# Turned RWKV product loops, inverses from blocks of 16, and two gate projections at another place in the order

## The chip, the cores and the metric

The kernel runs on one core of a Trainium2 chip, as one launch. The time is the device time of the launch in microseconds (us). TensorE (PE) multiplies, VectorE (DVE) and ScalarE (ACT) work elementwise and read the results out of PSUM, GpSimd (POOL) does elementwise work beside them, and SyncE (SP) issues the DMAs.

## The reference

One sequence of 512 tokens with 1024 features goes through two blocks. The first has one layer with two mixers, sparse attention (NSA, 8 heads) and RWKV-7 (8 heads of 64), each gated by a silu. The second block has two layers (differential attention, then gated linear attention), each with cross attention to a memory and a convolutional feed-forward. What the change touches is the RWKV mixer, whose reference is a scan over tokens:

```python
def rwkv7_step(state, inp):
    r_t, w_t, k_t, v_t, kk_t, a_t = inp
    sa = jnp.einsum('bhvk,bhk->bhv', state, -kk_t)
    state = (state * w_t[:, :, None, :] + sa[..., None] * (kk_t * a_t)[:, :, None, :]
             + v_t[..., None] * k_t[:, :, None, :])
    y = jnp.einsum('bhvk,bhk->bhv', state, r_t)
    return state, y
...
o_rwkv = o_rwkv * jax.nn.silu(g_rwkv.astype(jnp.float32))
```

## The kernel before

All matrix products with weights run as three half-precision products: weights and activations are split into a high and a low f16 part. `wahead` loads a weight block (128x1024 f32, `wst`) by DMA, ACT makes `whi` and DVE makes `wlo` from it. Inside a stretch named by `WPOOL` (from the first to the fifth step of `I`) `wlo` is made by POOL instead, after one more ACT pass. A 128-column projection is 24 matmuls of 512 columns into a PSUM bank `psp`: 7 with `whi`, 7 with `wlo`, 7 with the low activations, then three more.

The RWKV scan is done in chunks of 64 tokens. There are 4 pairs of heads (`f`), each with 2 heads (`hp`), and 4 blocks of 128 tokens (`tb`) with 2 chunks each (`c`); so 64 pairs of head and chunk, of which 32 stand side by side in the free dimension (`u`) and 2 in the partitions. The steps are:

- `rwkv_s1` (A0 to A3, one per `f`) makes, among others, the 64x64 matrices `LR` of each head and chunk, and at its end the first parts of `Y` and `KV`: for each `c` 16 products of 64x64 by 64 columns in f32 (lines 848 to 861), `hp` outermost, so that 8 products in a row write the same half of the partitions.
- `rwkv_inv` (I) inverts 64 unit-triangular matrices of 64x64. DVE transposes the two 32x32 diagonal blocks of each into `lx` (line 876), so that each partition holds one 32x32 system, solves them by 31 steps of forward substitution (lines 880 to 891: a product into `itmp` and a subtraction, in two groups of columns, so up to four instructions a step), and transposes back into `itmp` and `Tt` (lines 895 and 899). The block between the diagonal ones follows from small products on PE: 64 products of 32x32 by 32 columns at line 908 and 64 at line 920, in two halves each, `c` outside `u`.
- `rwkv_s2` (M) multiplies by these inverses (line 938, bank `psx` from `AX` and `Tt`) and then, for each `f` and `c`, makes 16 products of 64x64 by 64 columns into `pv` and 16 into `pv2` (lines 953 to 962), `hp` outermost.
- `rwkv_chain` (H) runs the recurrence over the 8 chunks, and `rwkv_s5` (F0 to F3) makes a gate projection, its silu (two POOL additions or products each) and the output's group norm.

Beside it run the NSA steps: K and C (keys and compressed keys), P0 to P3 (a pair of heads each: projection, scores `pss`, softmax on DVE and ACT, values `pso`) and G0 to G3 (gate projections and their silu). The list `ORDER` gives the order in which these steps are written; each entry advances its step to the next `yield`. What is written then goes through a scheduler, which moves instructions on each engine; the order that results is fixed, and each engine works it off one after the other. A wait of one instruction on PE is so a wait of everything behind it. In phase A there is one PSUM bank `x` (`psx`) and there are two of `psp`, three of `pss`.

A function `mm` (line 298) issues the matmuls; those of `rwkv_inv` are called on the engine directly and so have lines of their own. An f32 product is two records of PE in the trace (one weight load and one matmul each).

Of the kernel before, what the change touches and what calls it, by code (L numbers as in the profile page):

```python
# [18 lines left out]
NT = 4  # L19
# [7 lines left out]

ORDER = (
# [4 lines left out]
).split()  # L33
WKS = (1, 2, 6, 0, 3, 5, 4, 7)
# [2 lines left out]
DITEMS = "h0 c0 h1 h2 c1 h3 h4 h5".split()  # L37
LAG = 3
NDEPTH, NHL, NTT = 2, 3, 4
WPOOL = ('I.1', 'I.5')  # L40
DKS = (7, 1, 3, 2, 6, 4, 0, 5)
ICOLS = (0,7,32)
IPOOL = 9
GORDER = "m0 k q v0 v1 v2 m1".split()
GFILL = (4500, 1000, 0, 8500)
GKS = (1, 2, 0, 3, 6, 4, 7, 5)
# [4 lines left out]
def _const_table():  # L51

    p = np.arange(128)
    c = {}
    c["ident"] = np.eye(128)
    c["bones"] = (p[:, None] // 64 == p[None, :] // 64) * 1.0
    same = p[:, None] // 64 == p[None, :] // 64
    c["u_inc"] = same & (p[:, None] <= p[None, :])
    c["v_inc"] = c["u_inc"] / 16.0
    c["v_suf"] = (same & (p[:, None] > p[None, :])) / 16.0  # L60
# [165 lines left out]
class Kern:  # L226
# [521 lines left out]
    def rwkv_s1(self, f):  # L748
# [99 lines left out]
        for c in range(2):  # L848
            cr = slice(64 * c, 64 * c + 64)
            p = self.psx()  # L850
            pv = p.rearrange("p (a b v) -> p a b v", a=2, b=NT)
            for hp in range(2):
                rows = slice(64 * hp, 64 * hp + 64)
                for tb in range(NT):
                    vv = vT[cr, tb, 64 * hp:64 * hp + 64]
                    self.mm(pv[rows, 0, tb, :], vv, kT[cr, hp, tb, 1, :])
                    self.mm(pv[rows, 1, tb, :], khT[cr, tb, 64 * hp:64 * hp + 64], vv)
            yv = P["Y"][:, f, :].rearrange("p (b c t) -> p b c t", b=NT, c=2)
            self.act(yv[:, :, c, :], pv[:, 0], AF.Copy)
            kv = P["KV"][:, f].rearrange("p (b c) v -> p b c v", b=NT)  # L860
            self.act(kv[:, :, c, :], pv[:, 1], AF.Copy)


    def rwkv_inv(self):
        nc, ip = self.nc, self.tp
        P = self.rwt
        LR = P["LR"]
        LRu = LR.rearrange("p h b a t -> p (h b) a t")
        lx = self.T(ip, [128, 2, 32, 32], F32, "lx")
        LU, XT = lx[:, 0], lx[:, 1]  # L870
        X = XT.rearrange("p i t -> p t i")
        tmp = self.T(ip, [128, 1024], F32, "itmp")
# [4 lines left out]
        nc.gpsimd.memset(XT, 0.0)  # L877
        nc.gpsimd.memset(XT.rearrange("p a b -> p (a b)")[:, 0:1024:33], 1.0)

        for i in range(31):  # L880
            n = 31 - i
            for g, (c0, c1) in enumerate(zip(ICOLS, ICOLS[1:])):
                m = min(i + 1, c1) - c0
                if m > 0:
                    eng = nc.gpsimd if g == IPOOL else nc.vector
                    tv = tmp[:, 256 * g:256 * g + n * m].rearrange("p (a b) -> p a b", a=m)
                    self.tt(tv, LU[:, None, i + 1:, i].to_broadcast([128, m, n]),
                            XT[:, c0:c0 + m, i:i + 1].to_broadcast([128, m, n]), ALU.mult, eng)
                    self.tt(XT[:, c0:c0 + m, i + 1:], XT[:, c0:c0 + m, i + 1:], tv, ALU.subtract, eng)
            if i % 6 == 5:  # L890
                yield
        D = self.T(ip, [128, 1024], F32, "itmp").rearrange("p (u i) -> p u i", u=32)
        Tt = self.T(ip, [128, 32, 64], F32, "Tt")
        nc.gpsimd.memset(Tt, 0.0)
        nc.vector.transpose(out=D.rearrange("p u i -> p i u"), in_=X.rearrange("p t i -> p i t"))
        for q in range(4):
            r = slice(32 * q, 32 * q + 32)
            o = 32 * (q % 2)
            nc.vector.transpose(out=Tt[r, :, o:o + 32].rearrange("p u t -> p t u"), in_=X[r])
        E = LU  # L900
        for half in range(2):
            p = self.psx()
            pv = p.rearrange("p (u i) -> p u i", u=16)
            for c in range(2):
                a, b = slice(64 * c, 64 * c + 32), slice(64 * c + 32, 64 * c + 64)
                for u in range(16):
                    uu = half * 16 + u
                    self.nc.tensor.matmul(pv[b, u, :], lhsT=LRu[a, uu, 0, 32:64], rhs=D[a, uu, :], start=True,
                                          stop=True, tile_position=(64 * c, 64 * c + 32))
            for c in range(2):  # L910
                b = slice(64 * c + 32, 64 * c + 64)
                self.act(E[b, half * 16:half * 16 + 16, :], pv[b], AF.Copy)
        for half in range(2):
            p = self.psx()
            pv = p.rearrange("p (u i) -> p u i", u=16)
            for c in range(2):
                a, b = slice(64 * c, 64 * c + 32), slice(64 * c + 32, 64 * c + 64)
                for u in range(16):
                    uu = half * 16 + u
                    self.nc.tensor.matmul(pv[a, u, :], lhsT=E[b, uu, :], rhs=Tt[b, uu, 32:64], start=True, stop=True,  # L920
                                          tile_position=(64 * c + 32, 64 * c))
            for c in range(2):
                a = slice(64 * c, 64 * c + 32)
                self.act(Tt[a, half * 16:half * 16 + 16, 32:64], pv[a], AF.Copy, scale=-1.0)
        self.dump("Tt", Tt)
        self.Tt = Tt

    def rwkv_s2(self):
# [17 lines left out]
        for f in range(4):  # L946
            for c in range(2):
# [5 lines left out]
                for hp in range(2):  # L953
                    rows = slice(64 * hp, 64 * hp + 64)
                    h = 2 * f + hp
                    for tb in range(NT):
                        rb = LR[cr, h, tb, 1, :]
                        bh = Bh[cr, tb, h * 64:h * 64 + 64]
                        self.mm(pv[rows, 0, tb, :], WU[cr, h, tb, 0:64], rb)
                        self.mm(pv[rows, 1, tb, :], WU[cr, h, tb, 64:128], rb)  # L960
                        self.mm(pv2[rows, 0, tb, :], WU[cr, h, tb, 0:64], bh)
                        self.mm(pv2[rows, 1, tb, :], bh, WU[cr, h, tb, 64:128])
# [1002 lines left out]
```

## Time and profile before

| | us |
|---|---|
| three runs | 1648.43, 1652.76, 1655.37 (median 1652.76) |
| the profiled execution | 1650.08 |
| its span, first to last instruction | 1648.2 |
| PE busy | 1565.3 (95%) |
| DVE busy | 1039.3 (63%) |
| ACT busy | 759.9 (46%) |
| POOL busy | 231.4 (14%) |

PE is the busiest engine by far. Its slices in the page's second part are at 90% or more nearly everywhere; after the first slice the lowest ones are 7s, in the seventh (247 to 288 us) and the eleventh (412 to 453 us) of 40, and the line of the granted clock has an 8 and a 7 in the seventh and eighth. The seventh and eighth are the place of `rwkv_inv`. Phase A, with everything that the change touches, ends before 500 us. A line number in a row is that of the kernel before; line 298 is `mm`, 282 ACT's helper, 285 and 288 those of the two DVE (and POOL) forms.

### The profile page before, as it was taken

The page shows a single profiled execution, that of the slowest core. Times are in us where ns is not written, and L with a number is a line of the kernel's source. Part 1 is how long each engine was busy: PE and PEld are TensorE (multiplying, and loading weights), DVE is VectorE, ACT ScalarE, POOL GpSimd, SP SyncE. Part 2 cuts the span into 40 slices and gives each one's busy share as a digit, 9 for nine tenths or more (in the row PEclk, how much of TensorE's full clock was granted, in tenths as well). Part 3 has the DMA queues.
Part 4 walks back from the last instruction along what each step waited for, and adds up shares of the span by engine and source line. Part 5 has one row for each costly group of instructions (what it writes and reads, how often), then busy time and mean ns, then how long its engine had stood idle before and what let it go on. Part 6 is the DMA issues. An engine that isn't in the chain of part 4 may idle for free. (4 is left out here: it accounts for less than half of the span.)

```text
span 1648.2 us, 25438 instructions
## 1 busy us (share of the span) xinstructions
PE 1565.3 (95%) x9876; PEld 837.5 (51%) x9876; DVE 1039.3 (63%) x1908; ACT 759.9 (46%) x1399; POOL 231.4 (14%) x198
## 2 busy tenths in 40 slices
PE   6999997899799998899999999999999999999999
PEld 2465553576446665544444444456764444444444
DVE  6645779866755888876777763332476577777422
ACT  4443553454554777644444442225465444444211
POOL 2200124011141111221111110101000211111000
PEclk8999998799998999999999999999999999999999
DMA  5333441443453655533333333333224333333342
GB/s 186 99 106 97 100 103 37 87 81 72 95 162 110 162 147 129 132 98 102 100 100 101 100 102 101 106 92 97 65 59 115 103 102 103 101 101 100 111 125 64
DMA packets 133817, 171.06 MB, mean 104 GB/s; under 512 B 83471, under 2 KB 95680, under 8 KB 133697
## 3 DMA queue, kind: packets, MB, share of 16 engines
q1 hardware_dynamic: 133120, 168.39, 36.4%
q8 instruction: 77, 1.26, 0.3%
q10 hardware_dynamic: 576, 1.05, 0.2%
q14 instruction: 44, 0.35, 0.1%
HBM read 137.03 MB, written 3.28 MB: 85 GB/s over the span
## 5 line engine op out<-in xcount | busy, mean ns | idle before, releaser
L298 PEld LDWEIGHTS <-whi 128*128 128x128 f16 x3508 | 336.7, 98 | 401.4 <-issue 29.5
L285 DVE SCALAR_TENSOR_TENSOR wlo<-wst,whi 128x1024 f16<-128x1024 f32 (+2 forms) x250 | 306.9, 1228 | 255.6 <-ACT whi L282 255.0
L282 ACT ACTIVATE whi<-wst 128x1024 f16<-128x1024 f32 (+2 forms) x252 | 258.2, 1025 | 401.5 <-PE psp L298 328.6
L298 PE MATMUL psp<-hh,wlo 128*128 128x512 f16 x1112 | 296.6, 385 | 17.8 <-DVE wlo L285 17.8
L298 PE MATMUL psp<-hh,whi 128*128 128x512 f16 x1112 | 294.9, 381 | 10.6 <-ACT hh L282 6.3
L298 PE MATMUL psp<-hl,whi 128*128 128x512 f16 x1112 | 292.7, 381 | 0.0
L298 PEld LDWEIGHTS <-wlo 128*128 128x128 f16 x1754 | 170.9, 98 | 217.9 <-DVE wlo L285 19.0
L285 DVE SCALAR_TENSOR_TENSOR c<-ux,vecs,c 128x511 f32<-128x511 f32 (+1 forms) x176 | 133.2, 757 | 4.9 <-ACT c L282 1.8
L288 POOL TENSOR_TENSOR gl<-gg,gh 128x512 f16<-128x512 f32 x44 | 50.9, 1157 | 423.9 <-ACT gh L282 423.9
L298 PE MATMUL psp<-gh,wlo 128*128 128x512 f16 x352 | 91.6, 379 | 0.0
L298 PE MATMUL psp<-gl,whi 128*128 128x512 f16 x352 | 91.6, 379 | 0.0
L298 PE MATMUL psp<-gh,whi 128*128 128x512 f16 x352 | 91.6, 379 | 0.0
L288 POOL TENSOR_TENSOR acc<-acc,sq 128x512 f32<-128x512 f32 x34 | 53.0, 1564 | 220.2 <-ACT sq L282 220.2
L285 DVE SCALAR_TENSOR_TENSOR ux<-psp,rf 128x512 f32<-128x512 f32 x88 | 60.6, 688 | 32.6 <-PE psp L298 30.2
L282 ACT ACTIVATE c<-ux,vecs 128x512 f32<-128x512 f32 x88 | 70.3, 798 | 1.6 <-DVE ux L285 1.6
L282 ACT ACTIVATE c<-c 128x512 f32<-128x512 f32 x44 | 27.7, 629 | 91.6 <-DVE c L285 91.6
L298 PEld LDWEIGHTS <-hh 128*128 128x128 f16 x576 | 55.8, 98 | 19.8 <-issue 5.0
L298 PE MATMUL pso<-T,vh 128*64 128x128 f16 (+1 forms) x440 | 49.3, 224 | 13.2 <-DMA T<-hl 12.5
L282 ACT ACTIVATE pss<-pss,smst 128x128 f32<-128x128 f32 (+3 forms) x64 | 32.1, 501 | 51.1 <-DVE smst L293 45.5
L285 DVE SCALAR_TENSOR_TENSOR gg<-c,c 128x512 f32<-128x512 f32 x44 | 30.4, 692 | 34.8 <-ACT c L282 34.8
L298 PE MATMUL psp<-whi,hh 128*128 128x256 f16 (+3 forms) x240 | 51.3, 281 | 0.8 <-DVE kn L285 0.8
L298 PE MATMUL psp<-whi,hl 128*128 128x256 f16 (+3 forms) x240 | 51.7, 281 | 0.0
(452 smaller groups left out, 2230.9 us busy)
## 6 DMA issues: line engine op xcount, KB each, us to landing
wst<-in_w_up SPq DMA_DIRECT2D x88, 512.0 KB, 3.4
wst<-in_w_dn SPq DMA_DIRECT2D x32, 512.0 KB, 3.6
wst<-in_w_o SPq DMA_DIRECT2D x24, 512.0 KB, 3.6
wst<-in_w_rw SPq DMA_DIRECT2D x13, 512.0 KB, 3.3
wst<-in_w_dqk SPq DMA_DIRECT2D x12, 512.0 KB, 3.8
wst<-in_w_dn SPq DMA_DIRECT2D x16, 384.0 KB, 3.1
wst<-in_w_g SPq DMA_DIRECT2D x8, 512.0 KB, 3.6
wst<-in_w_dv SPq DMA_DIRECT2D x6, 512.0 KB, 4.2
```

The costliest lines, as they stand in the source:

```text
L282: return self.nc.scalar.activation(*a, **k)
L285: return self.nc.vector.scalar_tensor_tensor(out, in0, scalar, in1, op0=op0, op1=op1)
L288: return (eng or self.nc.vector).tensor_tensor(out, a, b, op=op)
L298: return self.nc.tensor.matmul(out, lhsT=lhsT, rhs=rhs, start=start, stop=stop, **kw)
```

## The change

Four things change. (1) The loops over 64x64 products at the end of `rwkv_s1` and in `rwkv_s2` are turned: the two heads of a pair alternate, so that neighbouring products write different halves of the partitions. The loops over 32x32 products in `rwkv_inv` are turned in the same way (`c` inside `u`). (2) The substitution works on blocks of 16 instead of 32. ACT copies the diagonal blocks into `LD` (4 copies of 32 partitions x 1024), DVE transposes them at once, 15 steps of two instructions each solve both 16x16 blocks (`r`) of a 32x32 system, and two further products on PE per system, 32x32 by 16 columns, give the block between them: 128 products at line 904 and 128 at line 914, which go round the four 32x32 quarters on the diagonal of the array. Between and around them stand two masked ACT copies (`B`, scaled by the new constant `m16`), DVE transposes, and at the end four ACT copies into `Tt`. (3) In `ORDER` F0, F1, G1 and G2 stand between the first and the second step of `I`. (4) `WPOOL` is empty: all `wlo` are made by DVE.

```diff
-    "... A3 F2 I F0 F1 I I I I P1 P1 P1 G1 P1 I P1 I "
-    "P1 P2 P1 P1 M ... P2 H P2 H G2 P2 P2 H P2 P3 "
+    "... A3 F2 I F0 F1 G1 G2 I P1 I P1 I P1 I P1 P1 "
+    "P1 P2 P1 P1 M ... P2 H P2 H P2 P2 H P2 P3 "
...
-WPOOL = ('I.1', 'I.5')
+WPOOL = ()
...
-            for hp in range(2):
-                rows = slice(64 * hp, 64 * hp + 64)
-                for tb in range(NT):
-                    vv = vT[cr, tb, 64 * hp:64 * hp + 64]
-                    self.mm(pv[rows, 0, tb, :], vv, kT[cr, hp, tb, 1, :])
-                    self.mm(pv[rows, 1, tb, :], khT[cr, tb, 64 * hp:64 * hp + 64], vv)
+            for tb in range(NT):
+                for hp, rows in halves:
+                    self.mm(pv[rows, 0, tb, :], vT[cr, tb, rows], kT[cr, hp, tb, 1, :])
+                for hp, rows in halves:
+                    self.mm(pv[rows, 1, tb, :], khT[cr, tb, rows], vT[cr, tb, rows])
...
-            nc.vector.transpose(out=LU[r], in_=LRu[r, :, 0, o:o + 32].rearrange("p u t -> p t u"))
+            self.act(LD[r], LRu[r, :, 0, o:o + 32], AF.Copy)
+        nc.vector.transpose(out=LU, in_=LD.rearrange("p u t -> p t u"))
...
-        for i in range(31):
-            n = 31 - i
...
+        for i in range(15):
+            n, m = 15 - i, i + 1
+            tv = it[:, 512:512 + 2 * n * m].rearrange("p (r a b) -> p r a b", r=2, a=m)
+            self.tt(tv, lu[:, :, None, i + 1:, i].to_broadcast([128, 2, m, n]),
+                    Xr[:, :, 0:m, i:i + 1].to_broadcast([128, 2, m, n]), ALU.mult)
+            self.tt(Xr[:, :, 0:m, i + 1:], Xr[:, :, 0:m, i + 1:], tv, ALU.subtract)
...
+        nc.vector.transpose(out=D.rearrange("p u c -> p c u"), in_=X.rearrange("p c r t -> p c (r t)"))
+        yield
+        for r in range(2):
+            self.act(B[:, :, 16 * r:16 * r + 16], D, AF.Copy, scale=m16[:, r:r + 1])
+        nc.vector.transpose(out=BT, in_=B)
...
+        for u in range(32):
+            for r, o, tp in quarters:
+                nc.tensor.matmul(pv[r, u, :], lhsT=LRu[r, u, 0, o:o + 32], rhs=B[r, u, 0:16], start=True, stop=True,
+                                 tile_position=tp)
+        self.act(E[:, :, 0:16], pv, AF.Copy, scale=m16[:, 1:2])
+        yield
...
+                nc.tensor.matmul(pv[r, u, :], lhsT=E[r, u, :], rhs=BT[r, u, 16:32], start=True, stop=True,
+                                 tile_position=tp)
+        self.tt(BT[:, :, 16:32], BT[:, :, 16:32], pv, ALU.subtract)
+        nc.vector.transpose(out=D, in_=BT)
...
+        for r, o, tp in quarters:
+            self.act(Tt[r, :, o:o + 32], BT[r], AF.Copy)
```

The turned loop of `rwkv_s2` has the same form as that of `rwkv_s1`.

First place, DVE at the end of the substitution. Before, the order on DVE is this (`lx` from `lx` and `itmp` is a step's subtraction, `wlo_2976` the low weights of the next projection on PE):

```order
L288 TENSOR_TENSOR lx_2712<-lx_2712,itmp_2713 128x2x23
...
L288 TENSOR_TENSOR lx_2712<-lx_2712,itmp_2713 128x7x8
L1142 TENSOR_REDUCE smst_2911<-pss_2904 128x2
...
L285 SCALAR_TENSOR_TENSOR wlo_2976<-wst_2973,whi_2975 128x1024
...
L895 STREAM_TRANSPOSE itmp_3037<-lx_2712 128x32x32
```

Now it is this (`wlo_2760`, `wlo_2797`, `wlo_2834` belong to the projections of F1, G1 and G2, `wlo_2870` to P1's):

```order
L877 STREAM_TRANSPOSE lx_2714<-lx_2714 128x1024
...
L284 SCALAR_TENSOR_TENSOR wlo_2760<-wst_2757,whi_2759 128x1024
...
L284 SCALAR_TENSOR_TENSOR wlo_2797<-wst_2794,whi_2796 128x1024
...
L284 SCALAR_TENSOR_TENSOR wlo_2834<-wst_2831,whi_2833 128x1024
...
L893 STREAM_TRANSPOSE lx_2714<-itmp_2715 128x16x32
L284 SCALAR_TENSOR_TENSOR wlo_2870<-wst_2867,whi_2869 128x1024
L898 STREAM_TRANSPOSE itmp_2715<-lx_2714 128x1024
```

Before, 88 instructions of the substitution stand between two instructions of other work on DVE; now low weights stand at four places among the 30 of the new one.

Second place, PE around the substitution. Before, PE comes to `wlo_2976` (P1's projection, `psp_3248`) after the high parts of two projections, and to the small products after that:

```order
L298 MATMUL psp_4148<-hh_134,whi_3244 128x512
L298 LDWEIGHTS wlo_2976
L298 MATMUL psp_3248<-hh_134,wlo_2976 128x512
...
L908 MATMUL psx_3045<-itmp_3037,x_61 32x32 x32
```

Now the last of the four gate projections (`psp_2873`, G2) is followed at once by the first new products, which read `B` (in `lx`), with two sets of scores (`pss`) between them and the second:

```order
L297 MATMUL psp_2873<-hh_134,wlo_2834 128x512
L297 LDWEIGHTS whi_2833
L297 MATMUL psp_2873<-hl_135,whi_2833 128x512
L904 MATMUL psx_2906<-lx_2714,x_61 32x16 x128
L297 LDWEIGHTS qr_2546
L297 MATMUL pss_3037<-kd_138_618,qr_2546 128x256
...
L914 MATMUL psx_3058<-itmp_2715,lx_2714 32x16 x128
```

G1's projection stood on PE before this wait in the old order too; it is G2's that has come from a later place.

## Rows read from the trace of the kernel before

**Rows 1.** Waits of PE over the whole span: total us, times, longest us

```profile
PE psp L298 <- DVE wlo L285: 17.8, 2, 17.5
```

**Rows 2.** Stretches of the span: busy us and instructions of each engine

```profile
core 0: us, PE busy (x) PEld busy (x) DVE busy (x) ACT busy (x) POOL busy (x), PEclk, DMA share, GB/s
255.50:276.90 21.40, 20.79 (x106) 9.57 (x103) 21.24 (x40) 8.74 (x14) 14.49 (x10) 1.00 0.22 56
276.90:294.40 17.50, 0.03 (x1) 0.00 (x0) 17.50 (x76) 2.62 (x9) 0.21 (x1) 0.58 0.00 0
294.40:300.40 6.00, 5.93 (x18) 2.35 (x19) 4.28 (x23) 1.81 (x4) 0.00 (x0) 0.51 0.85 175
310.60:317.40 6.80, 6.31 (x77) 4.71 (x75) 5.70 (x10) 3.51 (x9) 0.00 (x0) 0.50 0.31 92
342.00:404.00 62.00, 62.00 (x800) 46.70 (x801) 42.45 (x140) 24.56 (x63) 7.91 (x7) 1.00 0.40 73
404.00:454.00 50.00, 39.35 (x404) 22.50 (x404) 39.56 (x101) 29.80 (x66) 13.00 (x10) 1.00 0.40 83
```

**Rows 3.** PE in order of time: start, us, instruction, count, [idle before <- releaser]

```profile
255.56 1.67 PE L298 MATMUL psp<-hh,whi 128*128 128x512 f16 x7
...
260.74 1.67 PE L298 MATMUL psp<-hh,whi 128*128 128x512 f16 x7
...
275.25 1.69 PE L298 MATMUL psp<-hh,whi 128*128 128x512 f16 x7 [0.61 <-ACT whi L282]
294.47 3.17 PE L298 MATMUL psp<-hh,wlo 128*128 128x512 f16 x7 [17.54 <-DVE wlo L285]
```

**Rows 4.** DVE and POOL in order of time, during the substitution

```profile
264.98 3.38 DVE L288 TENSOR_TENSOR lx<-lx,itmp 128x66 f32<-128x66 f32 x2
266.10 2.12 POOL L288 TENSOR_TENSOR wlo<-wst,whi 128x1024 f16<-128x1024 f32 x1
...
289.62 0.41 DVE L288 TENSOR_TENSOR itmp<-lx 128x66 f32<-128x66 f32 x2
289.93 0.36 DVE L288 TENSOR_TENSOR lx<-lx,itmp 128x66 f32<-128x66 f32 x2
```

**Rows 5.** Stretches: busy us of the instructions that read or write lx

```profile
251.40:261.60 10.20, 0.00 (x0) 0.00 (x0) 7.82 (x4) 0.00 (x0) 1.12 (x2) 1.00 0.04 9
261.60:276.90 15.30, 0.00 (x0) 0.00 (x0) 14.88 (x33) 0.00 (x0) 0.00 (x0) 1.00 0.30 79
276.90:301.10 24.20, 0.00 (x0) 0.00 (x0) 16.71 (x78) 0.00 (x0) 0.00 (x0) 0.58 0.24 49
301.10:312.50 11.40, 1.64 (x33) 1.51 (x33) 10.53 (x5) 2.35 (x4) 0.00 (x0) 0.92 0.19 37
```

**Rows 6.** PE in order of time: products of 32x32, and short ones of 31 columns

```profile
303.36 2.11 PE L908 MATMUL psx<-itmp,x 32*32 32x32 f32 x64
...
312.49 1.91 PE L920 MATMUL psx<-Tt,lx 32*32 32x32 f32 x32 [0.49 <-DVE Tt L899]
...
321.62 0.18 PE L298 MATMUL psg<-kcl,qc 128*128 128x31 f16 x1
...
321.98 0.18 PE L298 MATMUL psg<-kcl,qc 128*128 128x31 f16 x1
```

**Rows 7.** Tile lx: the weight load of a 32x32 product, ns min/median/max

```profile
L920 PEld LDWEIGHTS psx<-Tt,lx x128: 101/108/153, 310.1 to 319.1; 32*32 32x32 f32 x128
```

**Rows 8.** PE in order of time: 64x64 products, halves alternating, then not

```profile
244.71 1.15 PE L298 MATMUL psx<-sG,kT 64*64 64x64 f32 x32
...
343.61 1.90 PE L298 MATMUL psx<-x,AX 64*64 64x64 f32 x32
```

**Rows 9.** DVE and ACT, 251.3 to 330 us, by shape: busy us, mean ns

```profile
L285 DVE SCALAR_TENSOR_TENSOR wlo<-wst,whi 128x1024 f16<-128x1024 f32 x3 | 3.8, 1268 | 0.0
L282 ACT ACTIVATE whi<-wst 128x1024 f16<-128x1024 f32 x5 | 5.3, 1058 | 0.0
```

**Rows 10.** DVE in order of time: a full transpose

```profile
301.22 1.92 DVE L895 STREAM_TRANSPOSE itmp<-lx 128x1024 f32<-128x1024 f32 x1
```

More of the change, by code (lines that the diff above doesn't have):

```diff
@@ L868, in rwkv_inv @@
         LRu = LR.rearrange("p h b a t -> p (h b) a t")
+        m16 = self.const("m16", ip)
         lx = self.T(ip, [128, 2, 32, 32], F32, "lx")
-        LU, XT = lx[:, 0], lx[:, 1]
-        X = XT.rearrange("p i t -> p t i")
-        tmp = self.T(ip, [128, 1024], F32, "itmp")
+        LU, LD = lx[:, 0], lx[:, 1]
+        it = self.T(ip, [128, 1024], F32, "itmp")
         for q in range(4):
@@ new lines, in rwkv_inv @@
+        nc.vector.transpose(out=D.rearrange("p u c -> p c u"), in_=X.rearrange("p c r t -> p c (r t)"))
+        yield
+        B, BT = LD, it.rearrange("p (u t) -> p u t", u=32)
+        for r in range(2):
+            self.act(B[:, :, 16 * r:16 * r + 16], D, AF.Copy, scale=m16[:, r:r + 1])
+        nc.vector.transpose(out=BT, in_=B)
+        quarters = [(slice(32 * q, 32 * q + 32), 32 * (q % 2), (32 * q, 32 * q)) for q in range(4)]
+        p = self.psx()
+        pv = p.rearrange("p (u i) -> p u i", u=32)
@@ new lines, in rwkv_inv @@
+        for u in range(32):
+            for r, o, tp in quarters:
+                nc.tensor.matmul(pv[r, u, :], lhsT=LRu[r, u, 0, o:o + 32], rhs=B[r, u, 0:16], start=True, stop=True,
+                                 tile_position=tp)
+        E = LU
+        nc.gpsimd.memset(E[:, :, 16:32], 0.0)
+        self.act(E[:, :, 0:16], pv, AF.Copy, scale=m16[:, 1:2])
+        yield
+        p = self.psx()
+        pv = p.rearrange("p (u i) -> p u i", u=32)
+        for u in range(32):
+            for r, o, tp in quarters:
+                nc.tensor.matmul(pv[r, u, :], lhsT=E[r, u, :], rhs=BT[r, u, 16:32], start=True, stop=True,
+                                 tile_position=tp)
@@ L893, in rwkv_inv @@
+        self.tt(BT[:, :, 16:32], BT[:, :, 16:32], pv, ALU.subtract)
+        D = LD
+        nc.vector.transpose(out=D, in_=BT)
         Tt = self.T(ip, [128, 32, 64], F32, "Tt")
         nc.gpsimd.memset(Tt, 0.0)
[L895 to L899, printed above, removed]
+        yield
@@ L900, in rwkv_inv @@
         E = LU
+        halves = [(c, slice(64 * c, 64 * c + 32), slice(64 * c + 32, 64 * c + 64)) for c in range(2)]
         for half in range(2):
@@ L903, in rwkv_inv @@
             pv = p.rearrange("p (u i) -> p u i", u=16)
[L904 to L911, printed above, removed]
+            for u in range(16):
+                uu = half * 16 + u
+                for c, a, b in halves:
+                    nc.tensor.matmul(pv[b, u, :], lhsT=LRu[a, uu, 0, 32:64], rhs=D[a, uu, :], start=True,
+                                     stop=True, tile_position=(64 * c, 64 * c + 32))
+            for c, a, b in halves:
                 self.act(E[b, half * 16:half * 16 + 16, :], pv[b], AF.Copy)
+        for r, o, tp in quarters:
+            self.act(Tt[r, :, o:o + 32], BT[r], AF.Copy)
+        yield
         for half in range(2):
@@ L915, in rwkv_inv @@
             pv = p.rearrange("p (u i) -> p u i", u=16)
[L916 to L923, printed above, removed]
+            for u in range(16):
+                uu = half * 16 + u
+                for c, a, b in halves:
+                    nc.tensor.matmul(pv[a, u, :], lhsT=E[b, uu, :], rhs=BT[b, uu, :], start=True, stop=True,
+                                     tile_position=(64 * c + 32, 64 * c))
+            for c, a, b in halves:
                 self.act(Tt[a, half * 16:half * 16 + 16, 32:64], pv[a], AF.Copy, scale=-1.0)
@@ L952, in rwkv_s2 @@
                 pv2 = p2.rearrange("p (a b t) -> p a b t", a=2, b=NT)
[L953 to L962, printed above, removed]
+                pair = [(slice(64 * hp, 64 * hp + 64), 2 * f + hp) for hp in range(2)]
+                bh = lambda tb, h: Bh[cr, tb, h * 64:h * 64 + 64]
+                for tb in range(NT):
+                    for a in range(2):
+                        for rows, h in pair:
+                            self.mm(pv[rows, a, tb, :], WU[cr, h, tb, 64 * a:64 * a + 64], LR[cr, h, tb, 1, :])
+                for tb in range(NT):
+                    for rows, h in pair:
+                        self.mm(pv2[rows, 0, tb, :], WU[cr, h, tb, 0:64], bh(tb, h))
+                    for rows, h in pair:
+                        self.mm(pv2[rows, 1, tb, :], bh(tb, h), WU[cr, h, tb, 64:128])
                 for dst, a in ((R, 0), (Y, 1)):
```

24 lines of the change are left out of this document (9 added, 15 removed), and 4 rows, old and new, of the table ORDER.

## The prediction

> **What bounds the kernel now.** I read the page's busy shares first: PE is at 95%, so a change counts by what it does to PE's work and to PE's idle time. Then the list of waits on PE. One wait stands out: 17.5 us in one piece, for a `wlo` of DVE [rows 1]. The timeline of PE shows where: its first matmul with those weights starts at 294.47, after 17.54 idle [rows 3]. In the same stretch DVE is busy all of 17.50 us and nothing else works [rows 2]: DVE is in the middle of the substitution, and the `wlo`, 1.27 us of work [rows 9], stands behind 88 instructions of it. The lesson is in the order of DVE, not in the `wlo`. Then the table of stretches: after the wait PE runs at 0.51 of its clock for 6 us, so a projection's matmuls take twice as long (7 in 3.17 us instead of 1.67) [rows 3]; it runs at 0.50 once more between 310.6 and 317.4, behind the small products [rows 2]. From 342 to 404, where `rwkv_s2` runs, PE is busy 62.00 of 62.00 us with DVE at 42.45, so there a shorter PE program is worth its time; from 404 to 454 PE has 39.35 of 50 and waits in small pieces for DVE and ACT, so there work taken from PE is worth little [rows 2].
>
> **The substitution on DVE.** Instructions on `lx` take 7.82 + 14.88 + 16.71 + 10.53 = 49.9 us of DVE in 120 instructions [rows 5]. The new one has two full transposes and one of 16x16 blocks before the first new product's result is used (1.92, 1.92 and, with half the elements, 1.0 [rows 10]) and 30 small instructions on 30 to 128 elements. Pairs on 66 elements without POOL beside them take 0.41 and 0.36, so 0.2 each [rows 4]; for larger ones I add in proportion and take 0.27 on average: 30 x 0.27 = 8.1 us. Beside POOL it is another matter: the pair on 66 that takes 0.36 alone takes 3.38 while POOL works on a `wlo` for 2.12, each instruction ending only when a POOL instruction ends [rows 4]. The POOL `wlo`s go, but the silus of F2, F0 and F1 (two POOL instructions each) stay beside it; I add 3 us. Three `wlo`s stand among the steps: 3 x 1.27 = 3.8. Ahead of it ACT has to make four copies of 1024 columns, 1.06 each by the same width [rows 9], between its other work, so DVE starts its steps at about 260, hardly earlier than in the trace. It ends at 260 + 8.1 + 3 + 3.8 = 274.9, with the transpose at 275.9 and the masked ACT copy (512 columns, half of 1.06) at 276.5.
>
> **The cover.** PE has four projections from where F2 ends. One takes 260.74 - 255.56 = 5.18 [rows 3], four take 20.7. With the end of `rwkv_s1` 1.4 earlier (below), PE starts F0 at 255.56 - 1.4 = 254.2 and is through F0, F1, G1 and G2 at 254.2 + 20.7 = 274.9, plus what it waits for the `wlo`s of F1 and G2, which stand behind steps of the substitution: 0.6 and 1.3, an estimate from the order and the durations above. So PE gets to the first new product at about 276.8, when its operand is just ready. That is the point of the change: of 17.5 us of waiting some 3.2 stay (1.9 for `wlo`s, 0.5 at the first product, 0.8 at the second, which needs ACT to empty the bank). PE's idle time falls by 14.3. G2's work, 5.2, only changes its place: it fills the hole and leaves a stretch where PE was full.
>
> **The clock.** The 6 us at half clock after the wait go, worth half of it: 2.9. The second low stretch, which follows on the small products, comes again, and since there are more of these I let it be some 4 us longer, or 2 us of PE time.
>
> **New products.** 128 at line 904 and 128 at line 914, two records each: 512 records. No row shows one of 32x32 by 16 columns that goes round four quarters. The nearest: 32 columns, same quarter again and again, 2.11 / 64 = 33 ns; the same at half clock in the later piece, 1.91 / 32 = 60 ns; half-precision matmuls of 31 columns with a weight load each, of which the first and the last of 15 are shown, 14 steps in 0.36 us, 26 ns [rows 6]. The lower bound is the 33 ns halved for the columns and quartered if all four quarters work at once: 4 ns, 2 us for all. The upper one is a weight load that nothing hides, 108 ns [rows 7], 55 us. I take 25 ns, from the 31-column row, since it is short in columns as these are: 12.8 us of PE. The Trainium skill's page "TensorE: Matmul & The Clock Gate" (Part 3: Packing small matmuls) has tiles at different places overlap with about 4 ns between starts, which would make the 512 records 2 us; its page "TensorEngine Tiling (Array Packing)" (Instruction Overhead) says that a matmul with one column takes as long as one with 60, and warns against tiling a dimension that is small already, which is 12.8 us and speaks against blocks of 16. The row of 31 columns agrees with the second, but its matmuls all use the whole array; no run here shows the first.
>
> **Turned loops.** 32 records of 64x64 by 64 columns take 1.15 us where neighbours write different halves, and 1.90 where they do not [rows 8]: 0.75 a group. `rwkv_s2` has 16 such groups, 12.0 us, `rwkv_s1` eight (two for each `f`), 6.0. The 256 records at the old lines 908 and 920 go from 33 or 60 ns to some 27: 3 us. Not all of it gets through. In `rwkv_s2`'s stretch PE falls from 62 to 62 - 12 - 5.2 = 44.8 us while DVE keeps 42.45 less one `wlo`: two engines that need nearly the same time and wait for each other through one bank. I let 5 us be lost there. In `rwkv_s1` PE waits now and then for DVE and DMA; I let 1.4 be lost. On the other side, if turning did nothing, 12 + 6 + 3 would go less the 6.4 that I don't count: 14.6 us.
>
> **ACT and POOL.** ACT gets eight copies of 1024 columns and three shorter masked ones, some 10 us, and loses two passes of 1.06; it is busy 8.74 of 21.4 us and 2.62 of 17.5 around there [rows 2], so this costs nothing by itself. What it costs in order: G1's silu on ACT stands behind the first masked copy, which waits for DVE; so G1's bank and the weights of P1 come later. PE has scores and the new products until then. If that cover went, a `wlo` of 1.27 and its `whi` of 1.06 would be late.
>
> **The sum**, against the profiled execution of 1650.1: idle -14.3, clock -2.9 + 2, new products +12.8, small old ones -3, `rwkv_s2` -12 + 5, `rwkv_s1` -6 + 1.4: -17.0, so 1633.1. That execution is 2.7 below the median of the runs, 1652.8; less 17.0 that is 1635.8. I forecast 1634, with a range of its own of 1626 to 1642.
>
> **Rivals.**
> - *The quarters work at once and the clock holds.* The alternating rows speak for overlap, the 26 ns of short matmuls against more of it. At 8 ns the products take 4 us, 9 less than in the sum; the clock's 2 go and half of what I took off for waiting, 3: 1634 - 14 = 1620. By the rule of 4 ns it would be 2 us less still.
> - *The small products run at half clock.* The stretch at 0.50 behind 303.36 speaks for it [rows 2, 6]; that short ones are held by something other than columns, against. At 53 ns (the 60 less the other work in it) 512 records take 27.1, 14 more: 1648.
> - *The substitution outlasts its cover.* POOL holds DVE longer than my 3 us, or the `wlo`s of F1 and G2 come later, as each stands behind five or more steps; then PE waits in front of the first product. With 9 us more on DVE and 3 for the clock behind such a wait: 1646. For it: 3.38 instead of 0.36 for one pair [rows 4]. Against: POOL's two `wlo`s are gone and G1's silu comes later.
> - *Slower: changing quarters lays the weight load bare.* If a record needs its load of 108 ns [rows 7] each time that the quarter changes, lines 904 and 914 take 55.3 instead of 12.8: 1676. The loads and products of 64x64 that alternate at 36 ns speak against [rows 8]. It decides from 25 + (17.0 + 8.3) / 0.512 = 74 ns a record on.
>
> **Chances.** Forecast 0.47, overlap 0.20, half clock 0.12, no cover 0.15, bare loads 0.06. About 0.5%, 8.3 us, is what a measurement of this kernel tells from no change; so faster is below 1644.5. The forecast and the overlap lie there whole, of the half clock a third (0.04) and of no cover 0.09: 0.80. Slower is the last rival, 0.06; the rest, 0.14, the same. The range goes from 1618, under the overlap's time, to 1649, over that of the half clock; it leaves out the bare loads, and the far ends of the others.
>
> **What would show it.** Right: the wait of 17.5 for a `wlo` is gone from the list; the 30 small instructions on `itmp` are over at about 275; line 904 starts within 2 us of G2's last matmul; 32 records of `psx<-x,AX` take 1.15. The record's price is read from lines 904 and 914, count over time. Wrong: a wait of over 5 us in front of line 904 (no cover), a clock of 0.5 across lines 904 and 914 with 50 ns or more a record (half clock), 100 ns a record at full clock (bare loads); or if PE, with `rwkv_s2` shorter by 12 us, waits for DVE just as much longer.

## The result, and the profile after

The changed kernel takes 1636.30 us (median of 4 runs, 1631.71 to 1638.84), the kernel before beside it 1653.88 (4 runs); the ratio is 0.9899, 95% interval 0.9871 to 0.9927. Timed again among the experiments it took 1635.60, ratio 0.9910 (0.9894 to 0.9926). So it is faster by 0.9 to 1.0%, 15 to 17.6 us; the forecast was 1634. The profiled execution took 1631.71 with a span of 1629.5, against 1650.1 and 1648.2 before.

The waits of PE first, as in [rows 1], here from 240 to 420 us (total us, times, longest):

```profile
PE pso L297 <- DMA T<-hl: 6.6, 8, 1.6
PE psx L914 <- issue: 4.0, 2, 2.1
PE psp L297 <- DVE wlo L284: 3.0, 1, 3.0
PE psx L904 <- issue: 2.4, 1, 2.4
```

The wait of 17.5 for a `wlo` is down to 3.0. New are 6.4 us at the two new products whose releaser is "issue": no semaphore, engine or buffer that the profile shows. Over the whole span PE's idle time is 79.8 us (1629.5 less 1549.7 busy), against 82.9 before: of the 14.5 us that the hole gave up, 6.4 are these stops, and some 7 more are waits that have come up in `rwkv_s2`'s loops (3.6 where there was nothing) and at the start of `rwkv_chain`. PE's busy time fell by 15.6. Where the stops lie is in PE's timeline, which answers [rows 3, 6] (start, us, instruction, count, [idle before <- releaser]):

```profile
267.24 1.67 PE L297 MATMUL psp<-hh,whi 128*128 128x512 f16 x7
271.89 2.52 PE L297 MATMUL psp<-hh,wlo 128*128 128x512 f16 x7 [2.97 <-DVE wlo L284]
...
277.04 0.38 PE L297 MATMUL psp<-hl,whi 128*128 128x512 f16 x1
277.35 1.91 PE L904 MATMUL psx<-lx,x 32*32 32x16 f32 x206
281.67 0.60 PE L904 MATMUL psx<-lx,x 32*32 32x16 f32 x50 [2.41 <-issue]
...
283.18 1.15 PE L914 MATMUL psx<-itmp,lx 32*32 32x16 f32 x71
286.22 1.90 PE L914 MATMUL psx<-itmp,lx 32*32 32x16 f32 x128 [1.89 <-issue]
290.22 0.98 PE L914 MATMUL psx<-itmp,lx 32*32 32x16 f32 x57 [2.10 <-issue]
...
295.97 1.40 PE L930 MATMUL psx<-lx,x 32*32 32x32 f32 x64
...
334.24 1.15 PE L297 MATMUL psx<-x,AX 64*64 64x64 f32 x32
```

Line 904 starts 0.3 us after G2's last matmul. Its first 206 records, each with a weight load of its own, take 1.91 us, 9 ns each; then PE stands still for 2.41 us in the middle of a product whose operands are all there. Line 914 stops twice more, and between its two stops lie 128 records, that is 128 loads and 128 matmuls. With the stops the products take 4.9 us (277.35 to 282.20) and 8.0 (283.18 to 291.20). A turned group of 32 records takes 1.15, where one took 1.90 [rows 8].

The stretches, as [rows 2] (us, busy us and instructions of PE, PEld, DVE, ACT, POOL, then the granted clock, DMA):

```profile
272.30:275.80 3.50, 3.50 (x10) 1.26 (x9) 1.88 (x5) 1.45 (x3) 0.00 (x0) 0.54 0.51 150
282.60:296.30 13.70, 9.71 (x291) 6.25 (x290) 5.91 (x16) 6.47 (x12) 0.64 (x1) 0.51 0.19 52
332.70:383.80 51.10, 47.49 (x769) 32.87 (x763) 39.24 (x136) 23.53 (x58) 4.87 (x4) 1.00 0.45 82
```

The clock is at its lower level (1.2 GHz, the half) in two places: just behind the 2.97 us wait, and from behind line 904 over line 914 into P2's projection. `rwkv_s2`'s stretch, 62.0 us full of PE work before, is 51.1 with 47.5 of PE. And the DVE steps beside POOL, to answer [rows 4]:

```profile
258.05 1.26 DVE L287 TENSOR_TENSOR itmp<-itmp 128x30 f32<-128x30 f32 x1
257.90 1.35 POOL L287 TENSOR_TENSOR acc<-acc,sq 128x512 f32<-128x512 f32 x1 [1.64 <-ACT sq L281]
...
273.04 0.21 DVE L287 TENSOR_TENSOR itmp<-itmp 128x30 f32<-128x30 f32 x1
```

The step on 30 elements that takes 0.21 alone takes 1.26 beside a silu on POOL. Four steps are held so, some 4 us; the last step ends at 273.25. Three `wlo`s stand among the 30 steps (at 256.91, 262.29 and 270.61), the fourth behind them, at 277.02.

### The profile page after: what moved, and what is told of

It is laid out like the page before. It is cut to its first block, busy times and chain, and to the rows that moved or that the text cites. A ratio compares the mean times of both kernels' runs of the same rounds, so it can differ in the third digit from the quotient of the medians.

```text
span 1629.5 us, 26397 instructions
## 1 busy us (share of the span) xinstructions
PE 1549.7 (95%) x10388; PEld 819.3 (50%) x10388; DVE 1010.7 (62%) x1826; ACT 768.9 (47%) x1408; POOL 227.4 (14%) x198
## 5 line engine op out<-in xcount | busy, mean ns | idle before, releaser
L297 PE MATMUL psp<-wlo,hh 128*128 128x256 f16 (+3 forms) x240 | 51.4, 281 | 0.0
```

Source lines behind the costliest of these rows:

```text
L297: return self.nc.tensor.matmul(out, lhsT=lhsT, rhs=rhs, start=start, stop=stop, **kw)
```

## Experiments: how much is each part worth?

Three kernels divide the change. The first keeps the new inverse (with its turned 32x32 products and its places in `ORDER` and `WPOOL`) and puts the loops of `rwkv_s1` and `rwkv_s2` back; the second is the kernel before with those loops alone turned; the third puts back `rwkv_s2`'s alone.

```
-            for tb in range(NT):
-                for hp, rows in halves:
-                    self.mm(pv[rows, 0, tb, :], ...)
-                for hp, rows in halves:
-                    self.mm(pv[rows, 1, tb, :], ...)
+            for hp in range(2):
+                for tb in range(NT):
+                    self.mm(pv[rows, 0, tb, :], ...)
+                    self.mm(pv[rows, 1, tb, :], ...)
```

> The changed kernel with the product loops of rwkv_s1 and rwkv_s2 in their old order. Theory A (the turned loops are worth most of the gain; the traces show rwkv_s1's stretch 5.4 us shorter, and rwkv_s2's 12.1 shorter, of which 5.2 is G2 that moved away): turning is worth 5.4 + 7 = 12.4, so this run comes out near 1636 + 12 = 1648, 5 us under the kernel before, and the groups of psx take 1.9 again. Rival B (waits for DVE and ACT swallow most of the shorter products; the gain is the hole of 17.5 us): 1640 to 1643, 11 us or more under the kernel before.

> The kernel before with only the loops of rwkv_s1 and rwkv_s2 turned. Theory A: 12 us faster than before, near 1641, with the wait of 17.5 for a wlo still in the list, somewhat longer since PE arrives earlier while DVE's substitution ends when it did: what rwkv_s1 gives (some 4 before that wait) is partly eaten by it, so 8 to 12 us. Rival B: at most 4 us. If the two parts don't interact, this gain and that of the run with the old loops add up to 17.6.

> The changed kernel with the old loops in rwkv_s2 alone (rwkv_s1's stay turned). If the stretch of rwkv_s2 shows the price, 8 us of the 15 that both are worth: 1644, with the first product of the chain (psx<-KV,lx) 8 us later than in the changed kernel. If more of the 15 is rwkv_s1's (which also brings PE 3 to 4 us earlier into the stretch of the substitution): 1640 to 1642. If nearly all is rwkv_s2's: 1648.

Measured against the kernel before: old loops 1648.55, ratio 0.9993 (0.9981 to 1.0004); only turned 1640.23, 0.9933 (0.9914 to 0.9952); old loops in `rwkv_s2` alone 1644.41, 0.9956 (0.9940 to 0.9972), beside the changed kernel's 0.9910 on the same chip. So turning is worth 0.7% alone and 0.8 to 0.9% on top of the new inverse, 11 to 15 us, of which `rwkv_s2` has 0.46%, 7.6 us (the chain's first product comes 8.6 us later, 394.5 against 385.9). Theory A holds, rival B is out. With the loops alone turned the wait for the `wlo` is 17.5 as before. The new inverse by itself is worth no more than the measurement tells, 0 to 3 us, and beside turned loops 0.2 to 0.3%, 4 to 6 us.

That is odd, since with the old loops the hole is gone as well (its longest wait for a `wlo` is 3.0). Where the gain goes is seen when the profiled runs are compared at the same points of the program: the first product of `rwkv_s2`'s loops (`psx<-x,AX`), the first one of `rwkv_chain` (`psx<-KV,lx`), the first one that reads `R` (`psp<-R,whi`), the first `psp<-mix,whi`, and the end (us from the span's start):

| | loops of `rwkv_s2` | chain | `psp<-R` | `psp<-mix` | end |
|---|---|---|---|---|---|
| before | 343.6 | 403.3 | 437.5 | 701.1 | 1648.2 |
| changed | 334.2 | 383.8 | 423.3 | 683.5 | 1629.5 |
| changed, second profile | 334.3 | 385.9 | 422.8 | 687.1 | 1633.4 |
| old loops | 337.6 | 395.3 | 433.0 | 698.5 | 1644.8 |
| only turned | 341.7 | 393.6 | 428.2 | 691.9 | 1639.0 |
| P2 between (below) | 336.8 | 384.6 | 422.9 | 688.6 | 1635.2 |
| halves (below) | 333.6 | 383.5 | 426.3 | 692.3 | 1638.8 |
| wide (below) | 323.1 | 375.2 | 416.1 | 682.2 | 1628.5 |

With the old loops the chain starts 8.0 us earlier than before, and at the first product with `R` 4.5 of them are left. Here is that stretch of the kernel before, of the one with old loops and of the changed one, and one of PE's waits in it, before and with old loops:

```profile
403.28:437.50 34.22, 28.05 (x360) 17.97 (x360) 28.27 (x85) 22.80 (x55) 8.42 (x6) 1.00 0.49 96
```

```profile
395.28:433.00 37.72, 28.34 (x370) 18.41 (x370) 30.93 (x93) 23.26 (x59) 5.66 (x6) 1.00 0.45 93
```

```profile
383.82:423.30 39.48, 29.80 (x371) 19.42 (x371) 30.68 (x93) 23.49 (x59) 6.36 (x6) 0.96 0.46 90
```

```profile
PE psx L298 <- DVE Y L288: 0.5, 1, 0.5
```

```profile
PE psx L297 <- DVE Y L287: 2.0, 2, 1.7
```

The clock is full in the first two and PE is busy alike; with old loops it waits 9.4 us instead of 6.2. So 3.5 of the 4.6 us that are lost go into waits at the start of the chain, most of them for DVE and ACT, and not into the clock. The changed kernel loses 5.3 us in the same stretch, 3.5 of it in waits, the rest at a clock of 0.96. All twelve profiles with the new inverse take 36.5 to 42.8 us here, the two with the old one 34.2 and 34.6. What lengthens these waits was not tested. The other place is the stretch up to `psp<-mix`, where the granted clock is 0.94 with the old loops from 587.8 to 698.5, and 0.97 before from 592.9 to 701.1, at 2.5 us. From `psp<-mix` to the end all fourteen profiles take 946.0 to 947.9 us.

## Experiments: what are PE's stops?

My theory, from the counts: PE takes its instructions in from memory by DMA, and two per record are more than come. The page's DMA table counts packets of a queue of the kind "instruction"; from 277.3 to 291.2, over both products, the changed kernel's trace has

```profile
q8 instruction: 3, 0.05, 1.7%
```

Three packets of 0.05 / 3 MB, some 16 KB each. 128 records between two stops are 256 instructions; 16 KB for 256 is 64 bytes for one. The Trainium skill's page "Trainium Architecture — The Big Picture" (The software stack) gives 64 bytes for an instruction; the trace agrees. PE goes on at 281.67, 286.22 and 290.22, so 256 instructions come in 4.0 to 4.6 us here, and the first 206 records ran on what had been fetched ahead. The trace has the time of each packet, and they bear the theory out: those three end at 280.45, 284.90 and 288.79, and PE goes on 1.2 to 1.4 us behind each. None ran between 260.53 and 279.03; from 260.53 to the first stop PE worked off some 520 records of loads and matmuls. The kernels of this document have 24 such stops of 0.2 to 2.9 us at these two products, and each one ends 1.2 to 1.5 us after a packet of this queue.

**Quarter outermost.** All 32 products of one quarter, then the next:

```
-        for u in range(32):
-            for r, o, tp in quarters:
+        for r, o, tp in quarters:
+            for u in range(32):
```

> The changed kernel with the quarter outermost at lines 904 and 914 (all 32 products of one quarter, then the next), everything else as it is. Theory F (PE's three stops of 2 us in the changed kernel are instruction fetch, 256 instructions in 4 us): at 33 ns a record, as the old small products showed, two instructions each, PE needs its instructions no faster than they come: no stop over 0.5 us, 512 records in 17 us, 4 us more than now, so 1640; up to 1646 if the clock falls to half for the second product. Rival O (rotating the quarters itself is what matters and the stops are something else): stops stay, and 20 ns more a record come on top, 10 us, so 1647.

It took 1649.35, ratio 0.9993 (0.9981 to 1.0004): the whole gain is gone. By line and shape (busy us, mean ns | idle before), this kernel, then the changed one:

```profile
L914 PE MATMUL psx<-itmp,lx 32*32 32x16 f32 x256 | 13.3, 209 | 0.0
...
L904 PE MATMUL psx<-lx,x 32*32 32x16 f32 x256 | 9.5, 187 | 0.0
```

```profile
L914 PE MATMUL psx<-itmp,lx 32*32 32x16 f32 x256 | 4.0, 210 | 4.0 <-issue 4.0
...
L904 PE MATMUL psx<-lx,x 32*32 32x16 f32 x256 | 2.5, 180 | 2.4 <-issue 2.4
```

No stop is left, as the theory said. A record takes 37 ns in line 904 (9.5 / 256, at a mean clock of 0.80) and 52 in line 914, all of it at half clock: the four quarters do work at once when one goes round them, and one alone doesn't hurry. I had priced this at 1640 to 1646. The two products take 22.8 us, 9.9 more than in the changed kernel, which is the upper end; 3 us more came behind them. The time is so nearer to rival O's 1647, but O's stops are not there.

**Pieces of 32 matmuls between P1's scores**, the same instructions in another order (in the kernels with another ORDER, lines have numbers a few lower: 901 for 904):

```
             for r, o, tp in quarters:
                 nc.tensor.matmul(...)
+            if u % 8 == 7 and u < 31:
+                yield
-ORDER: ... G1 G2 I P1 I P1 I P1 I P1 P1 P1 P2 P1 P1 M ...
+ORDER: ... G1 G2 I P1 I P1 I P1 I P1 I P1 I P1 I P1 I P2 I P1 P1 M ...
```

> The changed kernel with lines 904 and 914 in pieces of 32 matmuls (64 records, 128 instructions) and P1's scores, values and P2's projection between them; the same instructions in another order. Theory F (fetch): the large matmuls in between give the instructions time to come: the stops of 2.41, 1.89 and 2.10 fall to under 1.5 together, PE is better filled and the low clock from 282.7 to 296.3 is shorter; 5 to 8 us less than the changed kernel, 1628 to 1631. Rival O (the stops belong to the rotation of the quarters or to the writing of one bank): a stop of 2 us after every 128 records as before, and the same time or, for the broken-up scores, up to 4 more: 1636 to 1640.

It took 1647.86, ratio 0.9981 (0.9966 to 0.9997). On PE:

```profile
280.14 0.71 PE L901 MATMUL psx<-lx,x 32*32 32x16 f32 x63
281.49 0.17 PE L901 MATMUL psx<-lx,x 32*32 32x16 f32 x1 [0.64 <-issue]
...
284.26 1.03 PE L294 MATMUL psp<-hh,wlo 128*128 128x512 f16 x4
287.36 0.60 PE L294 MATMUL pss<-kd,qr 128*128 128x512 f16 x2 [2.07 <-DVE hl L281]
...
293.11 0.27 PE L294 MATMUL pso<-T,vh 128*64 128x128 f16 x1 [1.23 <-DMA T<-hl]
...
297.79 0.62 PE L913 MATMUL psx<-itmp,lx 32*32 32x16 f32 x30
```

Of the stops 0.64 is left: theory F on the stops is right, and rival O is out, since the quarters rotate as before. But the time is 12 us worse than the changed kernel's. P1's scores and values wait for DVE and for their transposes by DMA, and a piece of line 914 queued behind them on PE comes at 297.79, where the changed kernel is through at 291.20. `rwkv_s2`'s loops start at 338.5, 4.3 us later; the rest is lost behind. PE's instructions stand in one row: what is put between two pieces must itself be ready.

**Large matmuls between.** P2's projection, which waits for nothing, between lines 904 and 914; then also between the halves of line 904:

```
-ORDER: ... G1 G2 I P1 I P1 I P1 I P1 P1 P1 P2 ...
+ORDER: ... G1 G2 I P1 P2 I P1 I P1 I P1 P1 P1 ...
```

```
+            if u % 16 == 15 and u < 31:
+                yield
-ORDER: ... G1 G2 I P1 I P1 I P1 I P1 P1 P1 P2 ...
+ORDER: ... G1 G2 I P2 I P1 I P1 I P1 I P1 I P1 P1 P1 ...
```

> The changed kernel with the projection of P2 (24 large matmuls, 5.1 us, 48 instructions) between the products of line 904 and those of line 914, nothing broken up. Theory F (PE's stops are instruction fetch, 256 instructions in 4 us): the stop of 2.4 us after some 206 records of line 904 stays; in the 5.1 us instructions are fetched ahead, so line 914 runs some 175 records without a stop and has at most one more, up to 2 us, instead of two: 1633 to 1636, 0 to 3 us less than the changed kernel. Rival O (a stop after every 128 records, whatever stands between): three stops of 2 us as now.

> The changed kernel with lines 904 and 914 in two halves of 128 records each, and P2's projection (5.1 us of large matmuls) between the halves of line 904. Theory F: no stop in line 904 (128 records, then 5.1 us for the fetch, then 128), and at most one of 1 to 2 us in line 914; with the scores of P1 kept behind, the waits for their values that the kernel in pieces of 32 showed don't come. 4 to 6 us less than the changed kernel: 1630 to 1632, if the low clock after 282.7 becomes shorter with the stops. Rival W (what the stops cost is given back to the chain of P1's scores and values, or to DVE's later start of the next transpose, whatever the order): stops gone and 1636 to 1642.

The first took 1636.36, 0.9902 (0.9877 to 0.9927); the second 1642.31, 0.9936 (0.9911 to 0.9961). The second product of the first kernel, then the halves of the second:

```profile
291.86 0.83 PE L911 MATMUL psx<-itmp,lx 32*32 32x16 f32 x76
293.66 1.35 PE L911 MATMUL psx<-itmp,lx 32*32 32x16 f32 x82 [0.97 <-issue]
```

```profile
277.94 1.26 PE L901 MATMUL psx<-lx,x 32*32 32x16 f32 x128
279.13 1.68 PE L294 MATMUL psp<-hh,whi 128*128 128x512 f16 x7
...
292.13 0.95 PE L913 MATMUL psx<-itmp,lx 32*32 32x16 f32 x91 [1.90 <-issue]
```

In the first, line 914 runs 56 + 42 + 76 = 174 records and stops once for 0.97; theory F had said some 175. In the second, line 904 doesn't stop, and line 914 does once. So the stops are told by the count of instructions and by what runs between: rival O falls. Yet neither kernel is faster than the changed one, and the one with fewer stops is 6 us slower. DVE's transpose behind line 914, in the changed kernel and in the one with halves:

```profile
292.23 1.24 DVE L918 STREAM_TRANSPOSE lx<-itmp 128x1024 f32<-128x1024 f32 x1
```

```profile
294.66 1.23 DVE L919 STREAM_TRANSPOSE lx<-itmp 128x1024 f32<-128x1024 f32 x1
```

P2's 5.1 us stand ahead of line 914 and make it end later, though it stops less; with P2 between, this transpose starts at 296.38. So 4.5 us less in stops bring `rwkv_s2`'s loops 0.6 us forward with halves, and with P2 between they start 2.6 later (table above). That fits the second way that rival W names. The halves then lose 3.4 us more from the chain's first product to `psp<-R`, where the changed kernel's clock was 0.96:

```profile
383.45:426.30 42.85, 32.37 (x360) 20.32 (x359) 31.67 (x94) 22.65 (x56) 5.07 (x5) 0.88 0.45 81
```

**Fewer instructions.** One matmul of 64 columns in place of four of 16:

```
-        for u in range(32):
+        for u in range(0, 32, 4):
-                nc.tensor.matmul(pv[r, u, :], lhsT=..., rhs=B[r, u, 0:16], ...)
+                nc.tensor.matmul(pv[r, u:u + 4, :], lhsT=..., rhs=B[r, u:u + 4, 0:16], ...)
```

> The changed kernel with lines 904 and 914 as 32 matmuls of 32x32 by 64 columns instead of 128 by 16: one weight block serves four of the 32 blocks, so three quarters of the weight blocks are left out; everything else stays. It prices the number of instructions. Theory F (fetch): 128 records of at most 36 ns (as 64x64 ones that alternate), 1.3 to 4.6 us instead of 12.9, no stop: 8 to 11 us less up to the chain, 1625 to 1629. Rival (the products lie beside DVE's and ACT's chain, whose transposes and copies set the pace): at most 4 us less, 1632 to 1636, and PE waits for lx and Tt instead.

> The changed kernel itself once more, to have it on the same chip as the three beside it: 1636, within 3 us, with a mean granted clock between 0.980 and 0.986, and the three stops at lines 904 and 914 at the same records.

This kernel leaves out three quarters of the weight blocks, so it prices the instructions and computes something else. It took 1631.53, ratio 0.9889 (0.9871 to 0.9908), the changed kernel beside it 1635.60, ratio 0.9910 (0.9894 to 0.9926). No stop, 17 ns a record:

```profile
278.21 1.10 PE L904 MATMUL psx<-lx,x 32*32 32x64 f32 x64
...
281.07 1.10 PE L914 MATMUL psx<-itmp,lx 32*32 32x64 f32 x64 [0.38 <-ACT lx L281]
```

The chain's first product comes at 375.2, against 385.9 in the changed kernel's run beside it: 10.7 us, as theory F said. But the time is only some 4 us less, and the two intervals overlap. That is the rival's number and not for its reason: PE waits 0.38 for `lx`. Here the clock does take it: from the chain's first product to `psp<-R`, this kernel, then that other run:

```profile
375.23:416.10 40.87, 32.34 (x372) 20.95 (x371) 33.08 (x99) 22.73 (x58) 4.84 (x4) 0.87 0.41 79
```

```profile
385.91:422.80 36.89, 28.28 (x371) 18.46 (x371) 30.60 (x93) 23.37 (x59) 6.36 (x6) 1.00 0.45 95
```

PE waits alike, 8.5 and 8.6 us, and 4.0 us are lost at the lower clock. In the last stretch before `psp<-mix` (571.3 to 682.2, and 580.0 to 687.1 in the other run) it is 0.94 against 1.00, at 3.8 us more.

## Experiments: the cover, and the wait that is left

**G1 and G2 at late places in ORDER.**

```
-ORDER: ... F2 I F0 F1 G1 G2 I P1 I P1 ... P2 P2 H P2 H P2 P2 ...
+ORDER: ... F2 I F0 F1 I I P1 P1 P1 G1 P1 I ... P2 P2 H P2 H G2 P2 P2 ...
```

> The changed kernel with G1 and G2 put back to their late places in the table ORDER; the substitution's stretch then holds F0, F1, P1's scores and, pulled forward, G1; G2 falls back into the stretch of rwkv_s2. Theory C (four projections in a row are the cover that the substitution needs): PE waits 4 to 6 us more in front of line 904, with a low clock behind it, and G2's 5.2 us come back to a stretch that is no longer full: 1640 to 1645. Rival (P1's scores and G1 cover as well, the places of the projections don't matter): 1635 to 1638, the changed kernel's time.

1641.80, ratio 0.9930 (0.9911 to 0.9950): 5 us slower than the changed kernel, so the places matter, as theory C said; but the wait is another than it said. G1 is pulled forward and covers, too; what waits is a score of P1 that was drawn ahead of line 901. Its bank `pss` is read out only when DVE has made an `hl` of it, and that `hl` stands among the last steps of the substitution (274.62 to 275.23):

```profile
275.29 1.04 PE L294 MATMUL pss<-kd,qr 128*128 128x512 f16 x2 [6.47 <-DVE hl L281]
```

**G2's `wlo` on POOL**, and with P2's projection between the products:

```
-WPOOL = ()
+WPOOL = ('G1.1', 'G2.1')
```

> The changed kernel with the wlo of G2's weights made by POOL instead of DVE, so that it no longer stands behind 24 steps of the substitution. Theory D (the 2.97 us that PE waits for it, and the low clock behind it, cost what they show): PE gets through G2 3 to 4 us earlier and starts line 904 when its operand is ready, some 1.5 us earlier: 1632 to 1635. Rival L (POOL's 2.1 us hold DVE's steps that run beside them, as the trace before showed, and the substitution ends 1 to 2 us later): 1636 to 1638, with the wait in front of line 904 instead.

> The changed kernel with G2's wlo made by POOL (so PE doesn't wait 2.97 us for it) and with P2's projection between the products of lines 904 and 914 (so line 914 stops once, for 1 us, instead of twice for 4). If the two add up, by what their profiles show up to the end of rwkv_s2 (2.6 us earlier for the first, 3 us less in stops for the second): 1630 to 1633. Rival K (what PE gains here it gives back in a lower granted clock later on, as the kernel in halves did, whose mean clock was 0.978 against 0.983): 1635 to 1640, with the low stretches at other places.

The first took 1635.66, 0.9909 (0.9883 to 0.9935), the second 1640.31, 0.9932 (0.9913 to 0.9951). In the first:

```profile
269.02 1.69 PE L297 MATMUL psp<-hh,wlo 128*128 128x512 f16 x7 [0.96 <-POOL wlo L287]
...
274.91 2.39 PE L904 MATMUL psx<-lx,x 32*32 32x16 f32 x206 [2.05 <-ACT lx L281]
```

The wait of 2.97 is 0.96, and the gain of 2 us is nearly all given to the next wait, 2.05 for the masked copy at the end of the substitution; line 904 starts 2.4 us earlier, and the end doesn't move by more than can be told. For the second, rival K's number came: 5 us slower than the changed kernel beside it. Its mean clock was 0.982 in the median of six runs, against 0.982 there too, so the clock doesn't explain all of that. In its profile (its slowest run) `rwkv_s2`'s loops start at 336.9, 2.6 us later than in the changed kernel, with P2's projection ahead of line 911 as above; the rest stays open. No whole kernel here beats the changed one.

**How much the clock moves by itself.** The six runs of the kernel with P2 between go from 1628.49 at a mean clock of 0.992 to 1640.84 at 0.980, on one chip and for one program: 12 us. The medians of the mean clocks are 0.980 for the kernel before, 0.982 and 0.983 for the changed one, 0.978 for both that break up the products into pieces or halves. What decides where the low stretches fall was not found. The changed kernel's own two profiles differ as well, 0.96 and 1.00 from the chain's first product to `psp<-R`. So the profiles show what the low clock cost in one execution; that an edit between 277 and 300 us moved it is not shown by them, and the medians only hint at it.

## Why the prediction was right

The time and its sum were right, to 2 us; three terms of it were not, and one stretch had no term.

- **The hole.** Predicted: idle -14.3, with 3.2 left. The wait for the `wlo` fell by 14.5, the first product waits for nothing, and the cover of four projections holds. POOL held DVE by some 4 us, where I had added 3. The working of the cover has a slip: it lets F0 start 1.4 us earlier, but 1.4 is what it lets `rwkv_s1` lose, and its own terms give 6.0 - 1.4 = 4.6. Measured are 4.3 (251.24 against 255.56). So the cover began 3 us earlier than I took. That PE is through G2 at 277.3 all the same, near the 276.8 of the working, comes from the one `wlo` wait of 2.97, where I had 1.9 for two, and from the half clock behind it; the substitution was through earlier too.
- **The new products.** Predicted 12.8 at 25 ns a record; measured 12.9. This is the step that failed, with a right sum by luck: a record takes 9 ns, 15 at half clock (128 in 1.90 us), because the quarters do work at once, and 6.4 us are stops of instruction fetch, of which no step of mine spoke. The Trainium skill's page "TensorE: Matmul & The Clock Gate" (Part 3: Packing small matmuls) says that tiles at different places overlap, 4 ns from start to start. The trace agrees with the overlap, 9 ns with a weight load each against 37 when the quarter stays, though not with the figure. It speaks against the 25 ns that I took from a row of whole-array matmuls. The row to take was the 33 ns of [rows 6] over four quarters, which I had as the lower bound, 4 to 8 ns. The rival of overlap had the mechanism (8 ns) and the wrong time, 1620: with the stops it saves nothing, and without them the wide matmuls are 10.7 us earlier at the chain and some 4 at the end.
- **The clock.** Predicted -2.9 + 2. The low stretch behind the hole is not gone: it stands behind the 2.97 us that are left (272.3 to 275.8), and the one at the products has 9.71 us of PE's work in 13.7. That is 3.50 and 9.71 us at half clock, a loss of half, 6.6; before, 5.93 + 6.31 [rows 2], 6.1. So +0.5 instead of -0.9. Of the 9.71, 4.0 are line 914's own and stand in the 12.9 as well.
- **The old small products.** Predicted -3. They took 4.2 + 5.8 us before by line and take 2.6 + 2.4: -5.0.
- **Turned loops.** Predicted -7 for `rwkv_s2` with 5 of 12 lost, and -4.6 for `rwkv_s1`. Measured 7.6 for the one, and for both 11 (alone) to 15 us. The loss to the second engine is 3.6 us (PE has 47.5 of 51.1 there), where I had let 5 be lost.
- **The sum by parts.** For the inverse I had -14.3 - 0.9 + 12.8 - 3 = -5.4, for the loops -11.6. Measured 0 to -3 and -11 each alone, together -15 to -17.6. That is 3 to 5 us more than the two alone, about as much as their intervals leave open.
- **Behind `rwkv_s2`.** I had no term there, as if a lead at the chain's first product were a lead at the end. The profiles have 19.5 us of lead there (403.3 against 383.8), 14.2 at `psp<-R` and 18.7 at the end; in the second profile 17.4, 14.7 and 14.8. The stretch that I had called one in which work taken from PE is worth little takes back 3 to 5 us, in waits for DVE and ACT and in one profile by the clock. That the first profile gets 4.5 of its 5.3 us back further on is luck for the most part: 2.7 come from a stretch (499.3 to 507.2 before) where the kernel before had a clock of 0.65 and it had 1.00. With old loops 4.6 of the 8.0 us that the new inverse had brought are lost there and further on.

## What to carry to other kernels

A gap of "issue" in the middle of a run of small matmuls, after a like number of instructions each time, can be instruction fetch: count the instructions, and look whether each gap ends at the same distance behind a packet of the instruction queue. Work put between takes the stops away, but when it stands between two links of a chain it delays the chain by as much; no such order was faster here. Price a group of small products by how the neighbours share the array, not by the shortest instruction in the trace. And a gain in one stretch is only a gain at the end: compare two profiles at the same instructions, not at the same microseconds, tell waits from a lower clock in each stretch, and compare medians of several runs.

## What the runs showed of the hardware

- Weight load and matmul of 32x32 by 16 columns in f32 start every 9 ns when four quarters alternate (15 at half clock), every 37 at a mean clock of 0.80 when one is used again and again, 52 at half clock.
- PE's instructions came in packets of some 16 KB, 256 instructions in 4.0 to 4.6 us in the changed kernel; PE went on 1.2 to 1.5 us after a packet's end in all 24 stops. About 412 were at hand ahead of line 904 (206 records of two).
- Four DVE steps of 0.2 to 0.4 us took 1.1 to 1.35 beside a POOL instruction and ended within 0.15 us of its end.
- A program's mean granted clock differed from run to run between 0.979 and 0.992, at 12 us of time. In one stretch of 37 to 39 us the same program had 1.00 in one execution and 0.96 in another.
